# A hybrid decoder layer in float32: the first three weight blocks in ten pieces, and the unread matmuls on a constant

## The chip, the cores and the metric

The kernel runs on one core of a Trainium2 chip. The core has five engines that work side by side, each with its own instruction stream: TensorE (PE in the profile; its weight loads are shown apart as PEld), VectorE (DVE), ScalarE (ACT), GpSimd (POOL) and SyncE (SP), which here only issues transfers. Sixteen transfer engines move data between the device's memory and the on-chip memory. The metric is the device time of one execution in microseconds (us). The median of three runs is 1709.07 us (1709.02 to 1709.25).

## The reference

One layer of a decoder for 256 prompt tokens and 8 x 4 sample tokens, T = 288 rows of 2048 features, in float32:

```python
z = jnp.einsum('ntd,de->nte', x, w_in)
h, gate_b, gate_c, q, k, v, g_a, g_b = jnp.split(z, _split_points(), axis=-1)
ya = gate_b * causal_dwconv(gate_c * h)
yb = dilated windowed attention of q, k, v in 3 groups of 4 heads, merged
mixed = jax.nn.sigmoid(g_a) * (ya @ w_branch_a) + jax.nn.sigmoid(g_b) * (yb @ w_branch_b)
x1 = _layernorm(ALPHA * x + mixed @ w_out, ln1_g, ln1_b)
a, b = jnp.split(x1 @ w_up, 2, axis=-1)
y = _layernorm(ALPHA * x1 + (jax.nn.silu(causal_dwconv(a)) * b) @ w_down, ln2_g, ln2_b)
```

The lines for `ya`, `yb` and the convolution in `y` are shortened here. The key and value caches and the convolution states are returned as well. Nearly all the work is in the products with the weights: the weights are read once each, and the page counts 427.50 MB read in all.

## The kernel before

**Products.** Features lie on the 128 partitions. A weight matrix is cut into blocks of 128 output features; a block is 16 k-tiles (`KD`) of 128 x 128. So that TensorE keeps float32 accuracy, each operand is split into a rounded part `hi` and a remainder `lo` (`split`, line 248: ScalarE casts `hi`, VectorE subtracts to get `lo`). One k-tile of one block is then three matmuls of 288 columns: hi by hi, hi by the lo of x, and the lo of the weights by hi (`mms`, lines 243 to 245). A block is 48 matmuls.

**The usual stream of blocks.** `prepare` (line 185) issues the load of the next block from SyncE into the tile `wst` (three buffers) and splits it in two halves into `whi` and `wlo` (four buffers each). `product` (line 225) does a block. The first block that comes this way is called block 3 here; its load is issued in two halves (line 193).

**The front.** Blocks 0, 1 and 2 of the input projection don't go that way, since at the start both x and the weights are still on their way. Blocks 0 and 1 are loaded together into `w_two` (shown as the tile dd, its hi as yal, its lo as cache), block 2 into `w_one` (wst, whi, wlo), x into `xs` (yah, its hi as xh, its lo as xl). The front is cut into 8 pieces of two k-tiles (`N_PIECE`). For each piece three transfers are issued, x, `w_two`, `w_one` (lines 277 to 286), x from ScalarE's queue for the first two pieces and from SyncE's afterwards. ScalarE's table load is placed between its two (line 281, a copy of two columns of zeros). Then the casts and subtractions are written out and held in this order on ScalarE and VectorE (`casts`, `rests`, lines 287 to 310). In the first piece, x is cast one k-tile at a time, and VectorE does the cast of `w_two`, one k-tile at a time. `first_three` (line 314) runs the 144 matmuls of the three blocks piece by piece, in an order that is held: for each of the three terms, blocks 0 and 1, then block 2. `behind` (line 144) adds an order between two instructions of one engine.

**The unread matmuls.** Ahead of all this, TensorE runs `N_WARM` = 17 matmuls whose result nobody reads (line 261). They read a tile of zeros that VectorE writes (line 258).

**Behind the front** come the loads of block 3 (two halves), block 4, the constants (`cst`) and so on, all issued by SyncE (lines 195, 751, 390, 391).

Of the kernel before, what the change touches and what calls it, by code (L numbers as in the profile page):

```python
# [10 lines left out]
F32 = mybir.dt.float32  # L11
F32R = mybir.dt.float32r
# [5 lines left out]
P = 128  # L18
D = 2048
KD = D // P  # L20
# [3 lines left out]
T = SEQ + NS  # L24
# [8 lines left out]
HK = KD // 2  # L33
# [39 lines left out]
N_CT = 18  # L73
N_REST = 48

N_PIECE = 2

N_WARM = 17


PACE = 12, 13
# [19 lines left out]
def layer_kernel(ctx: ExitStack, tc: tile.TileContext, ins, outs):  # L101
    nc = tc.nc
    pe, dve, act, pool, sp = nc.tensor, nc.vector, nc.scalar, nc.gpsimd, nc.sync
# [3 lines left out]
    wk = ctx.enter_context(tc.tile_pool(name="wk", bufs=2))  # L107
    ps = ctx.enter_context(tc.tile_pool(name="ps", bufs=5, space=PSUM))
# [3 lines left out]
    def nm(s):  # L112
        uid[0] += 1
        return f"{s}_{uid[0]}"

    def sb(pl, shape, tag, dt=F32, bufs=None):
        return pl.tile(shape, dt, tag=tag, name=nm(tag), bufs=bufs)

    def acc(half=H):
        return sb(ps, [P, half, 2], "acc")  # L120
# [4 lines left out]
    def h3(ap):  # L125
        return ap.rearrange("p k (h a) -> p k h a", h=2)
# [8 lines left out]
    def f32(ap):  # L135
        return ap.bitcast(F32)
# [7 lines left out]
    def behind(i, after):  # L144

        tc.add_manual_dep(i.ins, after.ins.name, no_sync, reason="pace")
# [38 lines left out]
    def prepare():  # L185
        src, nk = next(w_left, (None, 0))
        if nk == 0:
            return
        st = sb(wp, [P, KD, P], "wst")
        src = src.rearrange("p (k c) -> p k c", c=P)  # L190
        loads[0] += 1

        for k0 in range(0, nk, HK if loads[0] == 1 else nk):
            k = slice(k0, k0 + (HK if loads[0] == 1 else nk))
            d = sp.dma_start(st[:, k, :], src[:, k])
        n = loads[0]
        w_load[0] = d
        if n >= 20 and n % 10 in (0, 3, 7):
            copy_rest(d)
        w_ready.append([half_block(st, k0, min(HK, nk - k0)) for k0 in range(0, nk, HK)])  # L200
# [24 lines left out]
    def product(x):  # L225

        w = w_ready.pop(0)
        if not w_ready:
            prepare()
        if steps_on[0]:  # L230
            next(steps, None)
        o = acc(x[0].shape[-1])
        mms(o, w, x)
        prompt_step()
        return o.rearrange("p a h -> p h a")
# [12 lines left out]
    def split(hi, lo, src):  # L248
        return act.copy(hi, src), dve.tensor_tensor(lo, src, f32(hi), ALU.subtract)  # L249

    ones_d = sb(big, [P, P], "ones_d", F32R)
    ones_p = sb(big, [P, P], "ones_p", F32R)
    pool.memset(f32(ones_d), 1.0 / D)
    pool.memset(f32(ones_p), 1.0 / P)


    zero = sb(wk, [P, T], "cy", F32R, bufs=2)
    dve.memset(f32(zero), 0.0)
    o = sb(ps, [P, T], "acc")
    for _ in range(N_WARM):  # L260
        pe.matmul(o, zero[:, :P], zero, start=True, stop=True)


    xh = sb(big, [P, KD, HX], "xh", F32R)[:, :, : 2 * HG].rearrange("p k (h a) -> p k h a", h=2)
# [1 line left out]
    x_in = ins["x"].rearrange("p (k t) -> p k t", t=T)  # L266
    xs = sb(big, [P, KD, T], "yah")
# [6 lines left out]
    w_one = sb(wp, [P, KD, P], "wst")  # L274
    w_one_hi, w_one_lo = ([sb(wp, [P, HK, P], n, F32R, bufs=4) for _ in range(2)] for n in ("whi", "wlo"))
    w_in_one = ins["w_in"][2].rearrange("p (k c) -> p k c", c=P)
    for k0 in range(0, KD, N_PIECE):
        k = slice(k0, k0 + N_PIECE)
        if k0 == N_PIECE:

            i_table = act.copy(sb(wk, [P, 2], "wgb", bufs=2), f32(zero[:, :2]))
        i_x = (act if k0 <= N_PIECE else sp).dma_start(xs[:, k], x_in[:, k])
        if k0 == N_PIECE:
            behind(i_x, i_table)
        sp.dma_start(w_two[:, :, k], w_in_two[:, :, k])
        sp.dma_start(w_one[:, k], w_in_one[:, k])
    casts, rests = [], []
    for k0 in range(0, KD, N_PIECE):
        k = slice(k0, k0 + N_PIECE)
        h = slice(k0 % HK, k0 % HK + N_PIECE)  # L290
        parts = (
            (xh[:, k, :, :H], xl[:, k, :, :H], xs[:, k].rearrange("p k (a h) -> p k h a", h=2)),
            (w_two_hi[:, :, k], w_two_lo[k0 // HK][:, :, h], w_two[:, :, k]),
            (w_one_hi[k0 // HK][:, h], w_one_lo[k0 // HK][:, h], w_one[:, k]),
        )
        for n, (hi, lo, src) in enumerate(parts):
            if k0 or n == 2:
                casts.append(act.copy(hi, src))
            else:

                for c in range(N_PIECE):
                    e = (slice(None),) * (1 + n) + (slice(c, c + 1),)
                    if n == 0:
                        casts.append(act.copy(hi[e], src[e]))
                    else:
                        rests.append(dve.tensor_copy(hi[e], src[e]))
        rests += [dve.tensor_tensor(lo, src, f32(hi), ALU.subtract) for hi, lo, src in parts]
    for row in (casts, rests):
        for before, i in zip(row, row[1:]):
# [4 lines left out]
    def first_three():  # L314

        prepare()
        o = [acc() for _ in range(3)]

        def first_w(lo, b, k):
            if b < 2:  # L320
                return w_two_lo[k // HK][:, b, k % HK] if lo else w_two_hi[:, b, k]
            return (w_one_lo if lo else w_one_hi)[k // HK][:, k % HK]

        before = None
        for k0 in range(0, KD, N_PIECE):
            for term in range(3):
                for blocks in ((0, 1), (2,)):
                    for k in range(k0, k0 + N_PIECE):
                        xk = x[term == 1][:, k].rearrange("p h a -> p a h")
                        for b in blocks:  # L330
                            i = pe.matmul(  # L331
                                o[b], first_w(term == 2, b, k), xk,
                                start=k == 0 and term == 0, stop=k == KD - 1 and term == 2,
                            )
                            if before is not None:
                                behind(i, before)
                            before = i
        return [t.rearrange("p a h -> p h a") for t in o]
# [23 lines left out]
    n = NH * NG * SEQ  # L362
# [373 lines left out]


    q_first = first_three()
    for j in range(NH):
        for g in range(NG):  # L740
# [12 lines left out]
    for j in range(NH):  # L753
        kT, vT = (kv[:, j % 2, c] for c in range(2))
        k_class = []
        for g in range(NG):
            for t in (kT, vT):
                o = product(x).rearrange("p h a -> p a h")
# [54 lines left out]
    for i in range(KD):  # L813
        ph = product(x)
        h = sb(wk, [P, T], "h", bufs=2)
# [19 lines left out]
    for i in range(KD):  # L835
# [3 lines left out]
        o = product((h3(yah), h3(yal)))  # L839
# [6 lines left out]
    for i in range(KD):  # L846
# [3 lines left out]
        o = product((h3(ybh), h3(ybl)))  # L850
# [182 lines left out]
    for i in range(KD):  # L1033
        o = product((h3(mxh), h3(mxl)))
# [35 lines left out]
    for part, nf in enumerate(THIRDS):  # L1070
# [42 lines left out]
        for i in range(KD):  # L1113
            o = product((h3(gh), h3(gl)))
# [209 lines left out]
```

## Time and profile before

| | |
|---|---|
| median of the runs | 1709.07 us |
| profiled execution, its own time | 1709.05 us |
| its span, first to last instruction | 1707.3 us |
| granted TensorE clock, mean | 0.999 |
| TensorE busy | 1699.9 us, 14148 matmuls |
| VectorE, ScalarE, GpSimd busy | 1192.2, 941.3, 387.6 us |
| moved by the transfer engines | 436.16 MB, 255 GB/s on average |
| transfer time, share of 16 engines' span, main queue | 67.6% |

How to read the rows that follow. A row of the timeline gives the start and the length in us, the engine, the line of the kernel, the operation, the tile written and the tiles read, the shape and the count of instructions that were merged into the row; in square brackets stands how long the engine had been idle before it, and what ended that. SPq and ACTq are the queues' own instructions, the issues of transfers. A row of the stretches gives for each engine the busy time and, in parentheses, the number of instructions. "us to landing" is the time from the start of an issue to the arrival of the last byte's signal. Sizes with KB are in units of 1024 bytes.

### The profile page before, as it was taken

How to read it: one execution, taken by the hardware profiler on the slowest of the kernel's cores; microseconds unless marked ns; L12 is line 12 of the kernel's file. 1: busy time of each engine (PE TensorE's matmuls, PEld its weight loads, DVE VectorE, ACT ScalarE, POOL GpSimd, SP SyncE). 2: the span in 40 equal slices, each digit the busy share in tenths (PEclk: the TensorE clock that was granted, in tenths of full speed). 3: DMA queues.
4: the chain of work that ended last, by engine and by line, in shares of the span. 5: the costliest groups of instructions: out<-in, count | busy, mean ns of one | idle time of the engine just before them, and what ended most of it. 6: DMA issues, size and time to landing. Idle time of an engine off the chain costs nothing.

```text
span 1707.3 us, 34334 instructions
## 1 busy us (share of the span) xinstructions
PE 1699.9 (100%) x14148; PEld 1694.4 (99%) x14148; DVE 1192.2 (70%) x1575; ACT 941.3 (55%) x1665; POOL 387.6 (23%) x510
## 2 busy tenths in 40 slices
PE   9999999999999999999999999999999999999998
PEld 9999999999999999999999999999999999999998
DVE  5477889978887675455788887855686554555575
ACT  5578876645666564444546555543555443344454
POOL 1123333202222210001453332300111100011164
PEclk9999999999999999999999999999999999999999
DMA  8788877676778886677766666666666566666663
GB/s 297 287 298 316 335 304 265 235 280 249 272 292 335 326 310 249 222 261 253 274 236 226 228 247 230 229 233 222 228 231 257 222 229 238 249 223 231 223 242 135
DMA packets 59068, 436.16 MB, mean 255 GB/s; under 512 B 7648, under 2 KB 11232, under 8 KB 19168
## 3 DMA queue, kind: packets, MB, share of 16 engines
q1 hardware_dynamic: 57472, 429.85, 67.6%
q10 hardware_dynamic: 1440, 4.13, 0.7%
q8 instruction: 110, 1.80, 0.4%
q14 instruction: 46, 0.38, 0.1%
HBM read 427.50 MB, written 94.53 MB: 306 GB/s over the span
## 4 chain that ended last, share of the span: by engine, by line
PE 98%; ACT 1%; DVE 1%; DMA 0%; issue 0%; SPq 0%; DVEq 0%
PE acc L243 32%; PE acc L245 32%; PE acc L244 32%; PE acc L331 1%; DMA wst<-in_w_in 0%; ACT yal L458 0%; DVE wlo L249 0%; PE acc L439 0%; PE att L478 0%; ACT yah L458 0%; ACT whi L249 0%; DVE dd L570 0%; PE long L978 0%; DVE yah L990 0%; PE acc L985 0%
## 5 line engine op out<-in xcount | busy, mean ns | idle before, releaser
L249 DVE TENSOR_TENSOR wlo<-wst,whi 128x1024 fp32r<-128x1024 f32 (+1 forms) x578 | 738.1, 1280 | 405.2 <-ACT whi L249 402.1
L249 ACT CAST whi<-wst 128x1024 fp32r<-128x1024 f32 (+1 forms) x578 | 588.6, 1021 | 679.9 <-PE acc L244 611.0
L243 PE MATMUL acc<-xh,whi 128*128 128x288 f32 (+1 forms) x3216 | 921.1, 286 | 0.0
L245 PE MATMUL acc<-xh,wlo 128*128 128x288 f32 (+1 forms) x3216 | 920.5, 286 | 0.4 <-DVE wlo L249 0.4
L244 PE MATMUL acc<-xl,whi 128*128 128x288 f32 (+1 forms) x3216 | 920.3, 286 | 0.0
L243 PEld LDWEIGHTS acc<-xh,whi 128*128 128x128 f32 x3216 | 607.8, 189 | 1.3 <-issue 1.2
L245 PEld LDWEIGHTS acc<-xh,wlo 128*128 128x128 f32 x3216 | 607.8, 189 | 0.8 <-DVE wlo L249 0.8
L244 PEld LDWEIGHTS acc<-xl,whi 128*128 128x128 f32 x3216 | 607.8, 189 | 0.0
L245 PE MATMUL acc<-yah,wlo 128*128 128x288 f32 x1216 | 347.7, 286 | 0.0
L244 PE MATMUL acc<-yal,whi 128*128 128x288 f32 x1216 | 347.7, 286 | 0.0
L243 PE MATMUL acc<-yah,whi 128*128 128x288 f32 x1216 | 347.6, 286 | 0.0
L245 PEld LDWEIGHTS acc<-yah,wlo 128*128 128x128 f32 x1216 | 229.8, 189 | 0.0
L244 PEld LDWEIGHTS acc<-yal,whi 128*128 128x128 f32 x1216 | 229.8, 189 | 0.0
L243 PEld LDWEIGHTS acc<-yah,whi 128*128 128x128 f32 x1216 | 229.8, 189 | 0.0
L794 POOL COPY qk_s<-u 128x2 f32<-128x2 f32 x44 | 36.8, 836 | 535.5 <-ACT u L1083 412.7
L782 DVE SCALAR_TENSOR_TENSOR cy<-u,prm,cy 128x304 f32<-128x304 f32 x120 | 72.6, 605 | 5.6 <-ACT cy L780 2.4
L564 POOL TENSOR_TENSOR cache<-cache,dd 128x1024 f32<-128x1024 f32 x16 | 34.1, 2134 | 93.4 <-DMA cache<-in_cv 55.8
L249 ACT CAST yah<-ya 128x288 fp32r<-128x288 f32 x76 | 32.6, 429 | 27.5 <-DVE ya L805 11.1
L564 POOL TENSOR_TENSOR cache<-cache,qk_s 128x1024 f32<-128x1024 f32 x16 | 32.7, 2045 | 53.7 <-DMA cache<-in_ck 40.6
L853 POOL TENSOR_TENSOR ya<-ya,dd 128x288 f32<-128x288 f32 x16 | 13.7, 858 | 133.8 <-DVE ya L852 132.8
L775 POOL COPY u<-prm 128x16 f32<-128x16 f32 x60 | 42.2, 704 | 4.6 <-DMA prm<-in_prm 4.6
L562 ACT ACTIVATE cache<-cache,qk_s 128x128 f32<-128x128 f32 x128 | 40.8, 392 | 0.0
(224 smaller groups left out, 1190.8 us busy)
## 6 DMA issues: line engine op xcount, KB each, us to landing
wst<-in_w_in SPq DMA_DIRECT2D x112, 1024.0 KB, 5.0
wst<-in_w_up SPq DMA_DIRECT2D x88, 1024.0 KB, 4.9
wst<-in_w_down SPq DMA_DIRECT2D x32, 1024.0 KB, 4.9
cache<-in_ck SPq DMA_DIRECT2D x18, 1024.0 KB, 7.8
cache<-in_cv SPq DMA_DIRECT2D x18, 1024.0 KB, 8.5
wst<-in_w_a SPq DMA_DIRECT2D x16, 1024.0 KB, 4.9
wst<-in_w_out SPq DMA_DIRECT2D x16, 1024.0 KB, 4.9
wst<-in_w_down SPq DMA_DIRECT2D x16, 768.0 KB, 4.4
```

The costliest lines, as they stand in the source:

```text
L243: pe.matmul(out, hi[:, c, :], xh_k, start=k == 0, stop=False)
L244: pe.matmul(out, hi[:, c, :], xl_k, start=False, stop=False)
L245: last_mm[0] = pe.matmul(out, lo[:, c, :], xh_k, start=False, stop=k == nk - 1)
L249: return act.copy(hi, src), dve.tensor_tensor(lo, src, f32(hi), ALU.subtract)
L331: i = pe.matmul(o[b], first_w(term == 2, b, k), xk, start=k == 0 and term == 0, stop=k == KD - 1 and term == 2,)
L562: behind(act.activation(o[:, a, b], t[:, a, b], AF.Copy, scale=w[:, a, b : b + 1]), w_split[0])
L564: behind(pool.tensor_tensor(o, t, w.unsqueeze(3).broadcast_to([P, *n]), ALU.mult), w_split[1])
L775: pool.tensor_copy(tail[:, :, 0:2], prm[:, state : state + 2 * NB].rearrange("p (b r) -> p b r", b=NB))
L782: dve.scalar_tensor_tensor(y, u[:, i : i + YW], prm[:, w0 + i : w0 + i + 1], y, ALU.mult, ALU.add)
L794: pool.tensor_copy(dst[:, 0:2], u[:, SEQ : SEQ + 2])
L853: pool.tensor_tensor(m, m, ma[:, i], ALU.add)
```

## The change

The front gets ten pieces, given as first k-tile and number of k-tiles: four of one k-tile, then six of two. All loops over the front go over this list. In the first piece, which is one k-tile now, x is cast in one instruction, and the cast of `w_two` stays on VectorE; all other casts are on ScalarE as before. The first two pieces' x is issued by ScalarE, the others' by SyncE. A piece of one k-tile takes x in rows of 1152 bytes and weights in rows of 512 bytes a partition, where a piece of two has 2304 and 1024. There are 30 transfers in place of 24.

The unread matmuls, now 15, read a constant zero that the program's preamble keeps in one column, with a step of zero over 128 and 288 columns. They stand ahead of GpSimd's two memsets in the program; VectorE's memset is gone. The copy that goes with the table load reads the same constant.

```diff
-N_PIECE = 2
-
-N_WARM = 17
+PIECES = (0, 1), (1, 1), (2, 1), (3, 1), (4, 2), (6, 2), (8, 2), (10, 2), (12, 2), (14, 2)
+
+N_WARM = 15
...
+    zero = nc.const_aps.tensor(0.0, [P, 1], F32)
+    zeros = [zero.bitcast(F32R).broadcast_to([P, n]) for n in (P, T)]
+    o = sb(ps, [P, T], "acc")
+    for _ in range(N_WARM):
+        pe.matmul(o, *zeros, start=True, stop=True)
     ones_d = sb(big, [P, P], "ones_d", F32R)
     ones_p = sb(big, [P, P], "ones_p", F32R)
     pool.memset(f32(ones_d), 1.0 / D)
     pool.memset(f32(ones_p), 1.0 / P)
-
-
-    zero = sb(wk, [P, T], "cy", F32R, bufs=2)
-    dve.memset(f32(zero), 0.0)
-    o = sb(ps, [P, T], "acc")
-    for _ in range(N_WARM):
-        pe.matmul(o, zero[:, :P], zero, start=True, stop=True)
...
-    for k0 in range(0, KD, N_PIECE):
-        k = slice(k0, k0 + N_PIECE)
-        if k0 == N_PIECE:
-
-            i_table = act.copy(sb(wk, [P, 2], "wgb", bufs=2), f32(zero[:, :2]))
-        i_x = (act if k0 <= N_PIECE else sp).dma_start(xs[:, k], x_in[:, k])
-        if k0 == N_PIECE:
+    for n, (k0, nk) in enumerate(PIECES):
+        k = slice(k0, k0 + nk)
+        if n == 1:
+
+            i_table = act.copy(sb(wk, [P, 2], "wgb", bufs=2), zero.broadcast_to([P, 2]))
+        i_x = (act if n <= 1 else sp).dma_start(xs[:, k], x_in[:, k])
+        if n == 1:
             behind(i_x, i_table)
         sp.dma_start(w_two[:, :, k], w_in_two[:, :, k])
         sp.dma_start(w_one[:, k], w_in_one[:, k])
     casts, rests = [], []
-    for k0 in range(0, KD, N_PIECE):
-        k = slice(k0, k0 + N_PIECE)
-        h = slice(k0 % HK, k0 % HK + N_PIECE)
+    for k0, nk in PIECES:
+        k = slice(k0, k0 + nk)
+        h = slice(k0 % HK, k0 % HK + nk)
...
         for n, (hi, lo, src) in enumerate(parts):
-            if k0 or n == 2:
+            if k0 or n != 1:
                 casts.append(act.copy(hi, src))
             else:
-
-                for c in range(N_PIECE):
-                    e = (slice(None),) * (1 + n) + (slice(c, c + 1),)
-                    if n == 0:
-                        casts.append(act.copy(hi[e], src[e]))
-                    else:
-                        rests.append(dve.tensor_copy(hi[e], src[e]))
+                rests.append(dve.tensor_copy(hi, src))
         rests += [dve.tensor_tensor(lo, src, f32(hi), ALU.subtract) for hi, lo, src in parts]
...
-        for k0 in range(0, KD, N_PIECE):
+        for k0, nk in PIECES:
             for term in range(3):
                 for blocks in ((0, 1), (2,)):
-                    for k in range(k0, k0 + N_PIECE):
+                    for k in range(k0, k0 + nk):
```

## The prediction

> **What bounds the kernel now.** I read the page first, for its span, its busy shares and its chain.
>
> ```profile
> span 1707.3 us, 34334 instructions
> PE 1699.9 (100%) x14148; PEld 1694.4 (99%) x14148; DVE 1192.2 (70%) x1575; ACT 941.3 (55%) x1665; POOL 387.6 (23%) x510
> ...
> PE 98%; ACT 1%; DVE 1%; DMA 0%; issue 0%; SPq 0%; DVEq 0%
> ```
>
> TensorE holds 98% of the chain, so the change can only act through the moment from which TensorE runs without a break. The stretches of the front show that moment (columns: stretch and its length, busy time and count of each engine, granted clock, DMA share, GB/s).
>
> ```profile
> 0.00:1.22 1.22, 0.00 (x1) 0.00 (x1) 0.30 (x1) 0.02 (x1) 0.62 (x8) 1.00 0.00 0
> 1.22:5.60 4.38, 4.31 (x18) 4.12 (x18) 0.44 (x3) 2.26 (x4) 0.00 (x0) 1.00 0.85 235
> 5.60:6.79 1.19, 0.73 (x4) 0.51 (x5) 1.19 (x3) 0.46 (x2) 0.00 (x0) 1.00 1.12 382
> 6.79:24.04 17.25, 17.25 (x140) 17.25 (x141) 13.66 (x25) 13.67 (x24) 0.15 (x1) 1.00 1.07 385
> ```
>
> The 17 unread matmuls fill 1.22 to 5.60, four real ones run, TensorE waits, and from 6.79 the other 140 of the 144 of `first_three` run to 24.04: 17.25/140 = 0.123 us each. Had all 144 run so, they would have begun at 24.04 - 144 x 0.1225 = 6.40. I call this the effective start. The chain of waits over the first 8 us says what sets it:
>
> ```profile
> 1.24 5.07 DMA wst<-in_w_in
> 6.31 0.02 issue
> 6.33 0.41 ACT whi L298
> 6.75 0.04 issue
> 6.79 1.25 PE acc L331 x8
> ```
>
> It is the landing of the first piece of `w_one` at 6.31, then its cast. After that the transfers stay close behind. ScalarE's timeline (start, length, what, idle time before it) shows this:
>
> ```profile
> 4.70 0.81 ACT L304 CAST xh<-yah 128x288 fp32r<-128x288 f32 x2 [2.02 <-DMA yah<-in_x]
> 6.33 0.40 ACT L298 CAST whi<-wst 128x256 fp32r<-128x256 f32 x1 [0.82 <-DMA wst<-in_w_in]
> 6.64 0.72 ACT L298 CAST xh<-yah 128x576 fp32r<-128x576 f32 x1
> ...
> 13.83 0.77 ACT L298 CAST xh<-yah 128x576 fp32r<-128x576 f32 x1 [0.20 <-DMA yah<-in_x]
> ...
> 15.72 0.76 ACT L298 CAST xh<-yah 128x576 fp32r<-128x576 f32 x1 [0.20 <-DMA yah<-in_x]
> ...
> 19.11 0.73 ACT L298 CAST xh<-yah 128x576 fp32r<-128x576 f32 x1 [1.72 <-DMA yah<-in_x]
> ...
> 21.50 1.04 ACT L249 CAST whi<-wst 128x1024 fp32r<-128x1024 f32 x1 [0.71 <-DMA wst<-in_w_in]
> ```
>
> Every piece waits for its x, and pieces come 15.72 - 13.83 = 1.89 us apart: the transfer engines, not TensorE (2 x 9 x 0.1225 = 2.2 us a piece), pace this queue. The next weights (block 3, line 195) stand in the same queue. Their first half is cast at 21.50, when it lands, and is subtracted on VectorE; the third matmul of block 3 reads the result:
>
> ```profile
> 22.58 2.50 DVE L249 TENSOR_TENSOR wlo<-wst,whi 128x1024 fp32r<-128x1024 f32 x2 [1.01 <-ACT whi L249]
> ```
> ```profile
> 24.17 0.19 PEld L245 LDWEIGHTS acc<-xh,wlo 128*128 128x128 f32 x1
> ```
> ```profile
> L249 DVE TENSOR_TENSOR wlo<-wst,whi x12: 1212/1224/1342, 22.6 to 48.7; 128x1024 fp32r<-128x1024 f32 x12
> ```
>
> The first of the two subtractions ends at 22.58 + 1.22 = 23.80, and the load of the weights begins at 24.17. With 0.04 us of hand-over (22.58 after the cast's end at 22.54) **the slack is 24.17 - 23.84 = 0.33 us**. This small number decides my forecast: an earlier front is worth no more than 0.33 us unless block 3 lands earlier too.
>
> **The change, part by part.** *The unread matmuls.* They now read a constant that is written in the preamble, so they no longer wait for VectorE.
>
> ```profile
> 0.24 0.10 POOL L1311 MEMSET const-float32-0.0<- 128x1 f32 x1 [0.24 <-issue]
> ...
> 0.73 0.20 POOL L253 MEMSET ones_d<- 128x128 f32 x1 [0.29 <-POOLq L1311]
> ```
> ```profile
> 0.87 0.30 DVE L258 MEMSET cy<- 128x288 f32 x1 [0.87 <-PEq L1311]
> ```
> ```profile
> 1.22 4.31 PE L261 MATMUL acc<-cy 128*128 128x288 f32 x17 [1.22 <-DVE cy L258]
> 5.60 0.73 PE L331 MATMUL acc<-xh,yal 128*128 128x288 f32 x4
> ```
>
> They can start when the other engines do, at 0.73 to 0.87 instead of 1.22, some 0.4 us earlier. Each takes 4.31/17 = 0.25 us, twice the later 0.1225, though the clock column reads 1.00 throughout; the four real ones behind them are nearly at full speed ((0.73 - 0.29)/3 = 0.15). Two fewer save 0.5 us: 15 end near 0.8 + 15 x 0.25 = 4.6. None lies on the path, as the first real operands come later. No row shows a matmul whose operands repeat one column; from below the price is zero, from above I take the longest of the unread ones, unpipelined, 0.607 us in the row below: 0.8 + 15 x 0.607 = 9.9 as their end. I take zero, because these are the same instruction with the same counts, and only the step differs.
>
> ```profile
> L261 PE MATMUL acc<-cy x17: 305/442/607, 1.2 to 5.2; 128*128 128x288 f32 x17
> ```
>
> *The small pieces at the front.* The queue's price per packet comes from two stretches, one of front pieces, one of whole blocks:
>
> ```profile
> DMA packets 2233, 2.75 MB, mean 366 GB/s; under 512 B 190, under 2 KB 1721, under 8 KB 2233
> ```
> ```profile
> DMA packets 407, 2.09 MB, mean 418 GB/s; under 512 B 45, under 2 KB 45, under 8 KB 209
> ```
>
> The first is 8.2 to 15.7 (16 engines x 7.5 us / 2233 = 53.7 ns a packet of 1232 B on average), the second 20 to 25 (80 us / 407 = 197 ns, 5135 B). A line through both is 8.6 ns a packet plus 0.0366 ns a byte. For the first piece, 480 of 960 KB stand before the end of its `w_one` (x of two pieces, `w_two`, `w_one`), in as many packets: 480 x 1024 x 0.0366 / 16 = 1.12 us earlier, a landing at 5.19. The cast of 128 columns is 0.27 (0.40 for 256, 0.72 for 576: 1 ns a column), so the first tile's third matmul starts at 5.50, two matmuls done before it: effective start 5.26, **1.1 us earlier**. Behind it ScalarE casts one tile at a time, 0.40 + 0.40 + 0.27 = 1.07 us against 1.10 of matmuls; it only just keeps up, so I count on 0.75 and keep 1.1 as the other end.
>
> The same four tiles cost the queue. Their weights go in 512-byte runs instead of 1024, x in 1152 instead of 2304: 256 more packets a tile, 1024 in all, and 6 more transfers with 16 completion packets each: 1120 x 8.6 / 16 = **0.60 us later for everything behind them**, block 3 included. From below this is 0 (only bytes count), from above 1120 x 53.7 / 16 = 3.8 us (only packets count). I take 0.60; the two stretches fix it.
>
> The Trainium skill speaks against this step: "DMA: Bandwidth & Descriptors" (Specifications) sets 512 B as the smallest transfer at line rate, so 512-byte runs would lose nothing; that is rival A below. The two stretches disagree already at 1024 and 2304 B: 366 against 418 GB/s.
>
> *Issue.* x came from ScalarE for the first two pieces before, too, so nothing changes engines; SyncE issues 28 transfers instead of 22.
>
> ```profile
> 4.70 0.33 SPq L286 DMA_DIRECT2D wst<-in_w_in  x1
> 5.15 0.38 SPq L282 DMA_DIRECT2D yah<-in_x  x1
> 6.33 0.38 SPq L285 DMA_DIRECT2D dd<-in_w_in  x1
> ```
>
> These are the 9th to 11th transfers; they start at the landings of the first three (x 4.70, `w_two` about 5.15, `w_one` 6.31). So eight are outstanding at once. In the new front eight hold 944 KB, or 2.6 us at 366 GB/s, against a shortest landing of 1.9:
>
> ```profile
> yal<-in_cst SPq DMA_DIRECT2D x4, 64.0 KB, 1.9
> ```
>
> So the queue should not run dry; if it does, SyncE's 0.33 to 0.47 us an issue gives at worst 1.3 us a tile against 0.94, over three tiles 1 us more. I take zero.
>
> *The casts of the first piece* move only with the piece. POOL's two memsets move behind the unread matmuls in program order, on another engine, and nobody in the front reads them.
>
> **The sum.** TensorE reaches block 3 at 24.04 - 0.75 = 23.29. Block 3's first half lands at 21.48 + 0.60, its subtraction ends at 24.40, and the load may begin at 24.44 instead of 24.17: **+0.27 us**. The 0.75 is swallowed by a wait of about a microsecond at block 3's third matmul. Behind that nothing passes the delay on: from 24.04 to 40.00 TensorE is busy without a gap,
>
> ```profile
> 24.04:40.00 15.96, 15.96 (x133) 15.96 (x132) 6.69 (x9) 6.85 (x14) 3.68 (x8) 1.00 0.62 213
> ```
>
> at a DMA share of 0.62, so the queue catches up there. The profiled execution took 1709.05 us (span 1707.3, and 1.75 around it), the median of the runs is 1709.07; 1709.05 + 0.27 = **1709.3**. About 0.2%, 3.4 us, is what a measurement can tell from no change: the forecast is no change.
>
> **The rivals.**
>
> *A: the runs of 512 B cost only their bytes.* Then block 3 lands when it does now and the slack caps the gain: -0.33, 1708.7. For it: nothing but bytes would matter; against it the two stretches. If moreover block 3 lands earlier, the lead itself is left, -0.75 to -1.1: 1708.0 to 1708.3. That could come from the one late engine:
>
> ```profile
> q8 instruction: 1, 0.02, 3.6%
> ```
>
> one instruction fetch (0.02 MB) shares the queue at 15.5 to 17.5, after which the x of the last piece is 1.72 us late instead of 0.20. Were it to fall elsewhere, block 3 would land up to 1.5 us earlier.
>
> *B, slower: TensorE is slow again.* The unread matmuls end at 4.6, the real ones begin near 5.2, and the half speed needs up to 4.3 us of unbroken work to go (1.22 to 5.5 above). If the gap counts as a break, the next 4.3 us run at half speed and lose 2.15: less the lead of 0.75, block 3 starts 1.4 us later than now, 1710.4. It decides from a loss of 0.75 + 0.27 = 1.02 us, eight or nine slow matmuls. For it: two fewer unread matmuls and an earlier start of them; against: the wait before 6.79 cost no speed.
>
> The Trainium skill ("TensorE: Matmul & The Clock Gate", Part 1: The HAM clock gate) has a free-running window of about 3.4 us that must be busy; by that an estimate of the loss is 1.7, and the time 1710.0.
>
> *C, slower: the queue runs dry or packets cost more than 8.6 ns.* Block 3 lands 1.0 us later on top, or up to 3.8 in all: 1710.3 to 1712.5.
>
> *D, slower: repeated columns read slowly*, 9.9 as the end of the unread ones: effective start 3.5 later than 6.40, 1712.6. Nothing in the profile speaks for it.
>
> **How the numbers follow.** Forecast (wait at block 3, 1709.0 to 1709.8) 0.50; A 0.20, of which 0.06 with the late engine gone; B 0.15; C 0.10; D 0.03; 0.02 for an order of instructions that changes further on. The range 1708.2 to 1711.0 leaves out the end of A with the full lead, the upper half of C and D. Only C's end, D and a changed order pass 3.4 us: slower 0.06, faster 0.03, the same 0.91.
>
> **What would show it.** Right: the first real matmul near 5.1 instead of 5.60; the first `w_one` cast near 5.2; pieces of two tiles still 1.9 us apart; the first cast of line 249 near 22.1; TensorE idle for some 1 us before the third matmul of block 3, with VectorE's subtraction (line 249) as releaser. Wrong: line 249's cast at 21.5 or before (A), real matmuls 0.25 us apart after 5.2 (B), DMA share under 1 between 5 and 10 us (C), unread matmuls beyond 5 us (D). A difference that arises behind 40 us would make the whole argument wrong.

## The result, and the profile after

| | before | after |
|---|---|---|
| median of 22 runs each, side by side | 1709.20 us (1707.76 to 1709.52) | 1711.47 us (1710.63 to 1712.86) |
| ratio, with its 95% interval | | 1.0015 (1.0009 to 1.0021) |
| profiled execution, its own time | 1709.05 us | 1711.30 us |
| its span | 1707.3 us | 1709.2 us |

The changed kernel is 0.15% slower. That is inside the 0.2% that the forecast called no change, but 2.3 us instead of +0.3, and outside the range, whose upper end was 1711.0. The last matmul of the profiled execution starts at 1703.82 instead of 1702.08, 1.74 us later. All of that arises in the first 45 us. Of the 2.25 us between the two own times 0.35 lies outside the span (2.1 us around it instead of 1.75) and some 0.2 behind the last matmul; neither was looked into.

TensorE's timeline of the new front shows the start and the first real matmuls, then the two long waits:

```profile
0.77 3.94 PE L255 MATMUL acc<-const-float32-0.0 128*128 128x288 f32 x15 [0.77 <-PEq L1303]
4.50 0.80 PE L323 MATMUL acc<-xh,yal 128*128 128x288 f32 x2
...
9.48 0.29 PE L323 MATMUL acc<-xh,wlo 128*128 128x288 f32 x1
11.32 0.76 PE L323 MATMUL acc<-xh,yal 128*128 128x288 f32 x4 [1.55 <-ACT yal L296]
...
14.13 0.76 PE L323 MATMUL acc<-xh,yal 128*128 128x288 f32 x4 [0.34 <-ACT yal L296]
```

The first real matmul runs at 4.50, 1.1 us earlier than before (5.60). Then TensorE works off the four small pieces and stands still ahead of the first piece of two k-tiles, until 11.32, and again ahead of the second, until 14.13. The stretches put sizes to that (columns as in the prediction):

```profile
4.50:9.60 5.10, 5.10 (x37) 5.05 (x36) 3.74 (x12) 3.08 (x10) 0.00 (x0) 1.00 0.93 253
9.60:11.32 1.72, 0.17 (x3) 0.00 (x1) 0.62 (x1) 1.36 (x3) 0.00 (x0) 1.00 0.84 264
11.32:25.26 13.94, 13.60 (x108) 13.38 (x109) 10.63 (x19) 10.33 (x18) 0.15 (x1) 1.00 1.03 380
```

The 36 matmuls of the small pieces take 5.10 us instead of 36 x 0.1225 = 4.41, because the first few run at half speed: 0.69 lost. The wait costs 1.72. The other 108 take 13.94 instead of 13.23: 0.71 lost, of which 0.51 is the wait before 14.13 (the piece before it ends at 13.62). Together 3.12 us, and the 144 are through at 25.26: 4.50 + 17.64 + 3.12. The effective start is 25.26 - 17.64 = 7.62, so the front is **1.22 us later** than the 6.40 of before, where 0.75 to 1.1 earlier was forecast.

The same stretches side by side tell where the bytes went, before first:

```profile
4.00:8.00 4.00, 3.47 (x21) 3.06 (x21) 2.71 (x6) 2.48 (x6) 0.00 (x0) 1.00 1.07 379
8.00:12.00 4.00, 4.00 (x35) 4.00 (x34) 3.85 (x8) 3.55 (x8) 0.00 (x0) 1.00 1.09 366
```

and after:

```profile
4.00:8.00 4.00, 4.00 (x26) 3.91 (x26) 3.33 (x11) 3.17 (x10) 0.00 (x0) 1.00 0.94 243
8.00:12.00 4.00, 2.45 (x20) 2.24 (x19) 2.16 (x6) 2.02 (x5) 0.00 (x0) 1.00 0.89 277
```

From 4 to 12 us the queue moves 243 and 277 GB/s instead of 379 and 366, 0.90 MB less. The DMA share is under 1 there. That is the sign the prediction had named for rival C. For the first of the two stretches SyncE's timeline shows why:

```profile
4.22 0.43 SPq L280 DMA_DIRECT2D yah<-in_x  x1
...
5.69 0.43 SPq L280 DMA_DIRECT2D yah<-in_x  x1
```

SyncE issues without a pause, three issues in 5.69 - 4.22 = 1.47 us, 0.49 each. A small piece is three issues and 144 + 128 + 64 = 336 KB: 344 kB / 1.47 us = 234 GB/s is all that SyncE can order, and 243 is what moved. A piece of two k-tiles gives 468 by the same sum, more than the engines carry.

The orders explain the first stretch and not the second. Summed over the packets of the traces, the bytes that are ordered and not yet moved are 0.44 to 0.98 MB from 4 to 7.5 us in the changed kernel, but 1.1 to 1.5 MB from 8 to 12, about what the kernel before has throughout (1.2 to 1.6). What differs is a few single packets: from 4 to 12 us 30 packets of the changed kernel (14 of them from 8 on) take over 0.25 us each, the longest 1.05, and only one does before (0.68). A landing counts when the last of its sixteen signals is in. Those of the x issued at 5.69 come from 8.21 to 9.94, spread over 1.73 us; before, the signals of each x that is issued in the first 9 us are spread over 0.82 to 0.85. That the long packets spread them is likely and not shown, and why they take so long, no run shows.

The x of the first larger piece, issued at 5.69, lands at 9.94, where the chain of waits has `DMA yah<-in_x` from 5.69 for 4.25 us; ScalarE's cast of it and of its weights leads to 11.32.

Everything behind it in the queue is late too. ScalarE's cast of block 3's first half, and TensorE at block 3:

```profile
23.20 1.04 ACT L249 CAST whi<-wst 128x1024 fp32r<-128x1024 f32 x1 [0.69 <-DMA wst<-in_w_in]
```
```profile
25.56 0.39 PE L245 MATMUL acc<-xh,wlo 128*128 128x288 f32 x1
25.79 0.29 PE L243 MATMUL acc<-xh,whi 128*128 128x288 f32 x1
...
43.19 0.29 PE L244 MATMUL acc<-xl,whi 128*128 128x288 f32 x1
43.55 0.39 PE L245 MATMUL acc<-xh,wlo 128*128 128x288 f32 x1
```

and before, block 3's fourth matmul:

```profile
24.41 0.29 PE L243 MATMUL acc<-xh,whi 128*128 128x288 f32 x1
```

The cast runs at 23.20 instead of 21.50, **1.70 us later** where 0.60 was forecast. There is luck in that figure: of this transfer's sixteen signals, fifteen are in at 22.42 instead of 19.85, 2.57 us later. The last one trails them by 1.63 us before and by 0.76 after; in both traces an instruction fetch shares the queue just ahead (from 16.29 and from 19.30). Block 3's third matmul waits a little (25.56 starts 0.05 late, and the next comes 0.23 behind it instead of 0.12), so block 3's fourth stands at 25.79 against 24.41: +1.38. A last wait, for another subtraction of line 249, comes at 43.2, from 43.19 to 43.55 with 0.10 more behind it: +0.34, hence +1.72. From there to the last matmul the two traces run in step.

### The profile page after: what moved, and what is told of

Same layout as the page of the kernel before. It is cut to its first block, busy times and chain, and to the rows that moved or that the text cites. A ratio compares the mean times of both kernels' runs of the same rounds, so it can differ in the third digit from the quotient of the medians.

```text
span 1709.2 us, 34350 instructions
## 1 busy us (share of the span) xinstructions
PE 1700.7 (100%) x14146; PEld 1694.8 (99%) x14146; DVE 1196.4 (70%) x1579; ACT 942.1 (55%) x1670; POOL 383.0 (22%) x510
## 4 chain that ended last, share of the span: by engine, by line
PE 96%; DMA 2%; ACT 1%; DVE 1%; SPq 0%; issue 0%; DVEq 0%; ACTq 0%
PE acc L243 32%; PE acc L245 32%; PE acc L244 32%; DMA wst<-in_w_in 1%; DMA yah<-in_x 0%; DMA dd<-in_w_in 0%; DVE wlo L249 0%; ACT whi L249 0%; ACT yal L450 0%; PE acc L431 0%; PE att L470 0%; ACT yah L450 0%; SPq L382 0%; DVE dd L562 0%; PE long L970 0%
## 5 line engine op out<-in xcount | busy, mean ns | idle before, releaser
L774 DVE SCALAR_TENSOR_TENSOR cy<-u,prm,cy 128x304 f32<-128x304 f32 x120 | 77.8, 648 | 5.6 <-ACT cy L772 2.4
```

Source lines behind the costliest of these rows:

```text
L774: dve.scalar_tensor_tensor(y, u[:, i : i + YW], prm[:, w0 + i : w0 + i + 1], y, ALU.mult, ALU.add)
```

## The experiments

Each was timed beside the kernel before on the same chip. Ratios have their 95% interval.

**1. The unread matmuls alone.** The kernel before, with 15 unread matmuls on the constant and the old pieces.

```diff
-N_WARM = 17
+N_WARM = 15
...
+    zero = nc.const_aps.tensor(0.0, [P, 1], F32)
+    zeros = [zero.bitcast(F32R).broadcast_to([P, n]) for n in (P, T)]
+    o = sb(ps, [P, T], "acc")
+    for _ in range(N_WARM):
+        pe.matmul(o, *zeros, start=True, stop=True)
...
-    dve.memset(f32(zero), 0.0)
```

> The kernel before, with only the unread matmuls changed (15 on the constant, no memset by VectorE). Theory (the loss is in the transfers of the small pieces): the first piece lands as before, TensorE reaches block 3 at 24.0 us, time within 0.3 us of the kernel before (1709.2). Rival B (half speed returns because the unread matmuls end at 4.5, a microsecond before the first real ones): real matmuls 0.25 us apart after 5.6, 1 to 2 us slower, 1710.2 to 1711.2.

Measured: 1710.72 against 1709.35, ratio 1.0006 (0.9997 to 1.0015). The 11 runs fall into two groups, three at 1709.2 to 1709.3 and eight at 1710.2 to 1711.2. The profiled one (1710.93) belongs to the upper group. TensorE's timeline of it:

```profile
0.77 3.59 PE L255 MATMUL acc<-const-float32-0.0 128*128 128x288 f32 x15 [0.77 <-PEq L1311]
5.63 0.73 PE L331 MATMUL acc<-xh,yal 128*128 128x288 f32 x4 [1.27 <-ACT xh L304]
6.81 0.51 PE L331 MATMUL acc<-xh,whi 128*128 128x288 f32 x2 [0.45 <-ACT whi L298]
7.16 1.05 PE L331 MATMUL acc<-xl,yal 128*128 128x288 f32 x4
```

and its stretches:

```profile
7.20:10.65 3.45, 3.45 (x17) 3.45 (x16) 3.32 (x7) 3.24 (x7) 0.00 (x0) 0.51 1.08 369
10.65:14.10 3.45, 3.45 (x29) 3.45 (x29) 3.12 (x7) 2.99 (x7) 0.00 (x0) 1.00 1.08 365
```

The 15 end near 4.4, 1.3 us before the first real operands, since the old first piece lands no earlier than it did. Four real matmuls then run fast, TensorE waits 0.45 us more, and from 7.2 to 10.65 the clock column reads 0.51: 17 matmuls where the next stretch of the same length has 29. That is the mechanism of rival B. It costs 12 x 0.1225 = 1.5 us. The theory of the expectation (within 0.3 us of before) holds in three runs, its rival B (1710.2 to 1711.2) in eight.

**2. The pieces alone.** The changed kernel with the old 17 unread matmuls on VectorE's zeros (the edit of experiment 1 backwards).

> The changed kernel with the old unread matmuls (17, VectorE's zeros). Theory: the stall at the first piece of two tiles stays, time within 0.5 us of the changed kernel (1711.5). Rival B: the half-speed matmuls at the start are gone and at least 1 us of the loss with them, 1710.5 or less.

Measured: 1710.95 against 1709.35, 1.0009 (1.0000 to 1.0018). The trace has 237 and 269 GB/s from 4 to 12 us, the wait ahead of the first two-tile piece (1.24 in the timeline, up to 11.78), and block 3's cast at 22.49. So the pieces carry most of the loss with either kind of unread matmuls: 1.60 us of it is left where the changed kernel loses 2.27, between the two expectations. Block 3's cast is 0.7 us earlier than in the changed kernel, with the same transfers. With one profile of each kernel, that 0.7 us can't be given a cause.

**3. Two small pieces instead of four.**

```diff
-PIECES = (0, 1), (1, 1), (2, 1), (3, 1), (4, 2), (6, 2), (8, 2), (10, 2), (12, 2), (14, 2)
+PIECES = (0, 1), (1, 1), (2, 2), (4, 2), (6, 2), (8, 2), (10, 2), (12, 2), (14, 2)
```

> The changed kernel with two pieces of one tile instead of four (nine pieces). Theory (SyncE's three issues of 0.48 us a tile feed the queue too slowly while the pieces are small, and it runs dry): pieces of two tiles follow after six issues, the queue stays full, no wait of TensorE over 0.3 us at the first piece of two tiles, block 3 lands about 0.3 us later than before instead of 1.7, 1708.8 to 1709.6. Rival (each small packet costs, whatever the queue): half of the loss stays, 1710.3.

Measured: 1710.12 against 1709.35, 1.0006 (0.9997 to 1.0015). No wait had been expected, but there was one:

```profile
7.07 0.29 PE L323 MATMUL acc<-xh,wlo 128*128 128x288 f32 x1
9.13 0.64 PE L323 MATMUL acc<-xh,yal 128*128 128x288 f32 x3 [1.77 <-ACT yal L296]
```

The two small pieces are used up at 7.19 and the first larger one is ready at 9.13. The queue moves 269 GB/s from 4 to 8 us and 381 from 8 to 12: six small transfers are enough to leave it short, only earlier and for less long. Block 3's cast comes at 22.08. The time lies nearer to the rival's 1710.3 than to the theory's 1708.8 to 1709.6, though in the trace the loss is the wait.

**4. Small pieces in the casts and matmuls, large ones in the transfers.** The changed kernel, whose loop over the transfers goes by two k-tiles again.

```diff
-    for n, (k0, nk) in enumerate(PIECES):
-        k = slice(k0, k0 + nk)
+    for n, k0 in enumerate(range(0, KD, 2)):
+        k = slice(k0, k0 + 2)
```

> The changed kernel with its ten pieces of casts and matmuls, but the eight transfers of two tiles that the kernel before has. Theory (the loss is in the transfers): the first real matmul waits for a landing at 6.3 again, no stall of more than 0.3 us later, time within 0.5 us of the kernel before, 1708.9 to 1709.7. Rival (the casts of one tile, 1.07 us a tile on ScalarE, hold TensorE up): more than 1 us slower than before.

Measured: 1710.68 against 1709.35, 1.0007 (0.9998 to 1.0016), again in two groups: four runs at 1709.0 to 1709.5, seven at 1710.7 to 1711.3. The profiled run (1709.46) is of the lower group. It moves 380 and 368 GB/s from 4 to 12 us, has block 3's cast at 21.51 as before (21.50) and no wait behind 7 us. So in this run shorter casts and matmuls cost nothing, and the transfers are what matters. The upper group takes the median out of the expected 1708.9 to 1709.7; it lies where that of experiment 1 does, and the unread matmuls again end 0.9 us or more ahead of the first real ones; no profile of that group was taken here.

**5. The packets alone.** The kernel before, with the weights of block 2 laid out in `wst` so that each run of a partition is 512 bytes: 1024 packets more, in the same 24 transfers.

```diff
-    w_one = sb(wp, [P, KD, P], "wst")
+    w_one = sb(wp, [P, KD, P], "wst").rearrange("p (a h) c -> p h a c", a=N_PIECE)
...
-        sp.dma_start(w_one[:, k], w_in_one[:, k])
+        sp.dma_start(w_one[:, k0 // N_PIECE], w_in_one[:, k])
...
-            (w_one_hi[k0 // HK][:, h], w_one_lo[k0 // HK][:, h], w_one[:, k]),
+            (w_one_hi[k0 // HK][:, h], w_one_lo[k0 // HK][:, h], w_one[:, k0 // N_PIECE]),
```

> The kernel before, with block 2's first weights stored so that all its eight transfers go in runs of 512 B instead of 1024: 1024 packets more, as many as the change adds, but no transfer more and no piece smaller. Theory: the queue is full, so the price is my 8.6 ns a packet, block 3 lands 0.55 us later (22.0 instead of 21.5) and the fourth matmul of block 3 starts about 0.2 us later than 24.41; time within 0.4 us of before. Rival (small packets are the loss): block 3 lands 1.7 us later as with the change, 1711.

Measured: 1709.38 against 1708.86, 1.0003 (0.9994 to 1.0013). Stretches, ScalarE and TensorE of its trace:

```profile
8.00:12.00 4.00, 4.00 (x35) 4.00 (x34) 3.75 (x8) 3.44 (x7) 0.00 (x0) 1.00 1.10 352
```
```profile
21.92 1.05 ACT L249 CAST whi<-wst 128x1024 fp32r<-128x1024 f32 x1 [0.76 <-DMA wst<-in_w_in]
```
```profile
24.28 0.39 PE L245 MATMUL acc<-xh,wlo 128*128 128x288 f32 x1
24.50 0.29 PE L243 MATMUL acc<-xh,whi 128*128 128x288 f32 x1
```

352 GB/s instead of 366, with the DMA share full. Block 3's cast is 0.42 us later, which is 0.42 x 16 / 1024 = 6.6 ns a packet (8.6 was forecast; by the fifteenth of the sixteen signals, 20.38 against 19.85, it would be 8.3). Its fourth matmul is 0.09 later, 24.50 against 24.41: 0.42 less the slack of 0.33. So the packets are dearer than their bytes, and they make a quarter of the 1.70.

**6. Four small pieces in the middle.** The same number of pieces, packets and transfers as in the changed kernel, at k-tiles 4 to 7.

```diff
-PIECES = (0, 1), (1, 1), (2, 1), (3, 1), (4, 2), (6, 2), (8, 2), (10, 2), (12, 2), (14, 2)
+PIECES = (0, 2), (2, 2), (4, 1), (5, 1), (6, 1), (7, 1), (8, 2), (10, 2), (12, 2), (14, 2)
```

> The changed kernel with its four pieces of one tile moved from tiles 0 to 3 to tiles 4 to 7; as many transfers and packets as the change. Theory: when the small pieces come, the queue holds 1.8 MB, SyncE is ahead, nothing runs dry; no wait of TensorE over 0.3 us at tile 8, block 3 lands 0.6 to 1.0 us later than before. Rival (small packets or casts, wherever they stand): block 3 lands 1.7 us later and TensorE waits at tile 8. The clock can add a window of half speed, seen as matmuls 0.24 us apart.

Measured: 1712.19 against 1708.86, 1.0019 (1.0010 to 1.0029). The expectation was that the transfers already ordered, 1.8 MB, would cover the small ones. They didn't: by the packets of the trace only 0.53 to 0.57 MB were ordered and not yet moved from 7.5 to 9 us, since no more than eight transfers are outstanding and the small ones fill these places. The stretches, and SyncE's timeline:

```profile
8.00:12.00 4.00, 4.00 (x35) 4.00 (x34) 4.00 (x13) 3.81 (x13) 0.00 (x0) 1.00 0.99 254
12.00:16.00 4.00, 3.05 (x25) 2.83 (x24) 1.13 (x4) 1.30 (x3) 0.00 (x0) 1.00 0.96 275
```
```profile
7.99 0.47 SPq L284 DMA_DIRECT2D wst<-in_w_in  x1
...
9.45 0.47 SPq L284 DMA_DIRECT2D wst<-in_w_in  x1
```

A piece in 1.46 us again (9.45 - 7.99), 236 GB/s ordered and 254 moved. The hole moves with the small pieces: TensorE waits at 16.30, ahead of the next large one (1.25 in its timeline), and block 3's cast runs at 23.72. So it is not the start of the kernel that is slow; small transfers are, wherever they stand. Here too the second stretch is slow with 1.1 to 1.3 MB outstanding.

**7. Smaller transfers, nothing else.** The kernel before, whose six transfers of the first two pieces are cut into two of 64 partitions each. The rows of each partition, the casts and the matmuls stay the same.

```diff
-        i_x = (act if k0 <= N_PIECE else sp).dma_start(xs[:, k], x_in[:, k])
+        at = (slice(0, P // 2), slice(P // 2, P)) if k0 <= N_PIECE else (slice(0, P),)
+        for h in at:
+            i_x = (act if k0 <= N_PIECE else sp).dma_start(xs[h, k], x_in[h, k])
...
-        sp.dma_start(w_two[:, :, k], w_in_two[:, :, k])
-        sp.dma_start(w_one[:, k], w_in_one[:, k])
+        for h in at:
+            sp.dma_start(w_two[h, :, k], w_in_two[h, :, k])
+        for h in at:
+            sp.dma_start(w_one[h, k], w_in_one[h, k])
```

> The kernel before, with each of the six transfers of the first two pieces cut into two of 64 partitions: twelve transfers of half the size, the same packets and the same pieces for the casts. Theory (issue rate and eight outstanding transfers): 0.45 us an issue at half the bytes lets the queue run dry between 4 and 8 us as in the changed kernel, DMA under 300 GB/s there instead of 370 to 390, and block 3 lands 0.7 to 1.5 us later. Rival (packet size): the same rate and the same landing as before, 21.5.

Measured: 1712.34 against 1708.86, 1.0021 (1.0012 to 1.0031). Stretches and SyncE:

```profile
4.00:8.00 4.00, 1.83 (x11) 1.38 (x10) 1.36 (x4) 1.19 (x4) 0.00 (x0) 0.96 0.86 197
8.00:12.00 4.00, 3.94 (x20) 3.94 (x21) 2.57 (x6) 2.44 (x6) 0.00 (x0) 0.62 0.78 223
```
```profile
0.73 1.51 SPq L288 DMA_DIRECT2D dd<-in_w_in  x2
...
3.68 1.29 SPq L288 DMA_DIRECT2D dd<-in_w_in  x2
6.55 1.13 SPq L290 DMA_DIRECT2D wst<-in_w_in  x2
```

197 and 223 GB/s with the old rows and the old pieces: the size and number of the transfers alone is enough. Here an issue takes 0.57 to 0.76 us, and between 4.97 and 6.55 SyncE waits 1.6 us for a landing. Block 3's cast runs at 26.12, 4.6 us later than before, where 0.7 to 1.5 was expected. This profiled run (1714.43) is the slowest of the ten by 1.7 us. Part of its loss is that its first piece is itself late (first real matmul at 7.08) and that half speed follows (0.62 in the clock column from 8 to 12); the size of the rest is not explained.

**8. x of the third and fourth piece from ScalarE.** The changed kernel with two issues fewer on SyncE.

```diff
-        i_x = (act if n <= 1 else sp).dma_start(xs[:, k], x_in[:, k])
-        if n == 1:
+        i_x = (act if n <= 3 else sp).dma_start(xs[:, k], x_in[:, k])
+        if 1 <= n <= 3:
```

> The changed kernel, x of the third and fourth piece issued by ScalarE too. SyncE has two issues fewer ahead of the first piece of two tiles, which it issues about 0.5 us earlier than 5.69. Theory: that piece's x lands 0.5 to 1 us earlier than 9.94 and the wait of 1.7 us there shrinks by as much; block 3 lands 0.3 to 0.8 us earlier than 23.2. Rival (packet size): both unchanged within 0.2 us.

Measured: 1710.92 against 1708.86, 1.0012 (1.0003 to 1.0022); no relief, against the expectation. SyncE's timeline:

```profile
2.23 0.47 SPq L284 DMA_DIRECT2D wst<-in_w_in  x1
3.74 0.38 SPq L283 DMA_DIRECT2D dd<-in_w_in  x1
...
5.15 0.47 SPq L284 DMA_DIRECT2D wst<-in_w_in  x1
6.63 0.33 SPq L280 DMA_DIRECT2D yah<-in_x  x1
```

Now SyncE stands still twice for a landing (2.70 to 3.74, 5.62 to 6.63), and x of the first large piece is issued at 6.63, later than 5.69. The limit has changed: it is the number of transfers outstanding instead of the time of an issue. Block 3's cast at 23.18 is where it was.

**9. One small piece in front.** Two k-tiles of the list are single, the first and one later, to keep the halves of the weights whole.

```diff
-PIECES = (0, 1), (1, 1), (2, 1), (3, 1), (4, 2), (6, 2), (8, 2), (10, 2), (12, 2), (14, 2)
+PIECES = (0, 1), (1, 2), (3, 2), (5, 2), (7, 1), (8, 2), (10, 2), (12, 2), (14, 2)
```

> The changed kernel with its ten pieces cut to nine: one tile first, then three pieces of two tiles, one of one, and four of two. Theory (small transfers run the queue dry, and the next x then comes slowly): only the first three transfers are small, 1.55 MB are issued by 3.7 us, the queue stays full, DMA at 350 GB/s or more from 4 to 16 us, x packets slow only before 4 us, block 3 lands within 0.4 us of before (21.5) instead of 23.2. Rival (the changed code of the front, whatever the transfers): block 3 still lands more than 1 us late. The time itself hangs on the clock, since TensorE waits for the second piece: 1709 to 1711.

Measured: 1708.52 (1708.08 to 1709.53) against 1709.10, 0.9998 (0.9989 to 1.0007). Stretches, ScalarE and TensorE:

```profile
4.00:8.00 4.00, 3.88 (x24) 3.52 (x24) 2.98 (x8) 2.69 (x7) 0.00 (x0) 1.00 1.05 360
8.00:12.00 4.00, 4.00 (x35) 4.00 (x34) 3.95 (x9) 3.28 (x8) 0.00 (x0) 1.00 1.08 358
```
```profile
20.95 1.05 ACT L249 CAST whi<-wst 128x1024 fp32r<-128x1024 f32 x1 [0.87 <-DMA wst<-in_w_in]
```
```profile
23.09 0.29 PE L243 MATMUL acc<-xh,whi 128*128 128x288 f32 x1
...
23.54 0.29 PE L243 MATMUL acc<-xh,whi 128*128 128x288 f32 x1
```

The queue stays full, block 3 starts at 23.09, 0.95 earlier than before, and its fourth matmul at 23.54, 0.87 earlier. That is more than the slack of 0.33 allows, because block 3's cast is 0.55 earlier (a landing within 0.4 of before was expected). That part looks like luck and not like the change: thirteen of the sixteen signals of block 3's first half are in at 19.77, as before (19.79), and only the last one, which trails behind the instruction fetch, comes earlier (20.93 instead of 21.48). It is what rival A had named for the late engine. The profiled run took 1708.08, below the expected 1709 to 1711, but seven of the 27 runs of the kernel before lie at 1708.0 to 1708.3 too, and the time can't be told from no change.

**10. 20 unread matmuls.** Experiment 1 with 20 instead of 15.

> The run with only the unread matmuls changed, but 20 of them on the constant instead of 15, so that they reach to the first real ones at 5.6. If the half speed there came from the gap of 1.3 us behind the unread matmuls: no real matmul 0.24 us apart after 7 us, all runs within 0.5 us of the kernel before, none near 1711. If it came from the constant or from the earlier start: the half speed stays, and two groups of times as before.

Measured: 1709.09 (1708.15 to 1709.29) against 1709.10, 1.0000 (0.9992 to 1.0009). The upper group of experiment 1 is gone, with the same constant. So the half speed there comes from the gap behind the unread matmuls, not from what they read. The two experiments ran on different chips, but experiment 7, on the chip of this one and with the old zeros, shows half speed behind a gap as well (2.01 us in its timeline).

**11. The slack alone.** The kernel before, with x of the second piece issued by SyncE behind the first weights, and block 3's first half cast and subtracted in quarters, so that its third matmul needs less of it.

```diff
-        i_x = (act if k0 <= N_PIECE else sp).dma_start(xs[:, k], x_in[:, k])
-        if k0 == N_PIECE:
-            behind(i_x, i_table)
+        (act if k0 == 0 else sp).dma_start(xs[:, k], x_in[:, k])
...
-        w_split[:] = split(hi[:, :n, :], lo[:, :n, :], st[:, k0 : k0 + n, :])
+        n_cast = 4 if loads[0] == 1 else n
+        for c in range(0, n, n_cast):
+            at = slice(c, c + n_cast)
+            w_split[:] = split(hi[:, at, :], lo[:, at, :], st[:, k0 + c : k0 + c + n_cast, :])
```

> The kernel before with x of the second piece issued by SyncE behind the first piece's weights, and the first half of block 3 cast and subtracted in quarters of four tiles. Theory: the first w_one lands 0.8 to 1.1 us earlier than 6.31, no transfer is smaller, block 3 lands as before, its first lo is ready 1.2 us earlier; TensorE is at block 3 0.4 to 0.8 us earlier than 24.04, 1708.3 to 1708.8. If the slack at block 3 were not the bound, the quarters would change nothing; if x of the second piece is late, TensorE waits there and the time stays.

Measured: 1708.64 (1708.31 to 1708.92) against 1709.10, 0.9998 (0.9989 to 1.0007). Block 3 starts at 23.67 and its fourth matmul at 24.04, without a wait and 0.37 earlier than before, the whole lead of its front. The quarters are not shown to be needed for it: in this profile block 3's cast begins at 20.86, 0.64 earlier than before, since the last of the sixteen signals trails less again (20.84 behind a fifteenth at 19.89), and that alone would have freed the slack. In time it can't be told from no change either.

## Why the prediction was wrong, step by step

**The step that failed is the one on issue:** "So the queue should not run dry; if it does ... over three tiles 1 us more. I take zero." Both halves of its working were too kind. It set eight outstanding transfers (944 KB) against "a shortest landing of 1.9", from one load of 64 KB of the constants. In the new front the same size takes longer. The list of DMA issues of the changed kernel, over the first 9 us (KB each, median us to landing):

```profile
dd<-in_w_in SPq DMA_DIRECT2D x4, 128.0 KB, 3.2
...
yah<-in_x SPq DMA_DIRECT2D x2, 144.0 KB, 3.2
wst<-in_w_in SPq DMA_DIRECT2D x4, 64.0 KB, 2.9
```

Eight transfers of 344 / 3 = 115 kB on average in 3.2 us are an estimated 287 GB/s, under the 366 that the engines carry. And "0.33 to 0.47 us an issue" counted the issues without the 0.04 to 0.05 us between them and with the shortest ones: 1.47 us a piece instead of 1.3, 234 GB/s. Either limit leaves the queue short while the small pieces are on their way. Experiment 8 lifts the one and meets the other, experiment 7 shows that smaller transfers do it without any other edit, experiment 6 that another place only moves the hole, experiment 3 that two small pieces make a smaller one, experiment 4 that nothing else in the pieces costs, and experiment 9 that one small piece at a time is carried. What follows had no term in the sum either: the long packets, with which the queue stays slow from 8 to 12 us although it holds enough again. At block 3 both together are 1.70 - 0.42 x 1120 / 1024 = 1.24 us where zero was taken, by single profiles and with the luck of the last signal in it. The short queue is the first half of rival C, to which the prediction gave one chance in ten; it named block 3 as the place, whereas the larger part of the loss is TensorE's own wait in the front (1.72 + 0.51).

**The lead at the start came, and larger than forecast.** The first real matmul was forecast near 5.1 and came at 4.50, the first cast of `w_one` near 5.2 and came at 4.24; why a whole microsecond earlier was not looked into. The lead was lost afterwards: TensorE works off a small piece in 9 x 0.1225 = 1.10 us where SyncE takes 1.47 to order one, and the x of the first larger piece then took 4.25 us to land.

**The unread matmuls cost what was taken:** 15 in (4.50 - 0.77) / 15 = 0.249 us each, against 0.25 before, with a column that repeats. Rival D falls.

**The price of a packet was right** within a third (6.6 ns against 8.6), and rival A falls with experiment 5. The Trainium skill's figure in "DMA: Bandwidth & Descriptors" (Specifications), 512 B as the smallest transfer at line rate, would have put experiment 5 at no loss; its 352 against 366 GB/s decides against it here, by 4%.

**The slack was right,** and it is the most solid number of the sum. From the start of block 3's first cast to its fourth matmul it is 2.59 us in the changed kernel (25.79 - 23.20), 2.58 in experiment 5 (24.50 - 21.92) and 2.59 in experiment 9 (23.54 - 20.95), wherever this chain binds. Before, it was 24.41 - 21.50 = 2.91, that is 0.33 more than needed: the 0.33 of the prediction.

**"Behind that nothing passes the delay on" was wrong by 0.34 us,** at 43.2. The share of 0.62 from which it was argued is a mean over 16 us; with block 3's data 1.70 late instead of 0.60, one subtraction was still late there. Without it the sum would be +1.38.

**Rival B is real, but not what decides here.** Experiment 1 shows its mechanism, half speed that returns behind a gap. In the profiled run of the changed kernel there is no such gap: the unread matmuls reach to the first real one, and the first five real ones, up to 5.81, still run at the half speed of the start, which makes the 0.69 us. Whether other runs of it lose more was not seen: what its runs lose beyond the 1.74 us of the trace (2.27 in the medians) is not placed.

**What stays open.** How the two limits and the long packets share the loss in the changed kernel. And where the long packets come from: from 8 to 12 us the changed kernel's DMA view has

```profile
DMA packets 916, 1.11 MB, mean 277 GB/s; under 512 B 74, under 2 KB 725, under 8 KB 916
```

and before, in the same stretch,

```profile
DMA packets 1206, 1.47 MB, mean 366 GB/s; under 512 B 105, under 2 KB 942, under 8 KB 1206
```

Both are packets of 1.2 kB on average, but the engines are busy 16 x 4 us x 0.89 / 916 = 62 ns with one instead of 16 x 4 x 1.09 / 1206 = 58. The packets don't all become slower: 14 of the 916 take over 0.25 us, and without these the mean is 55. From 4 to 12 us the traces of experiments 2, 3, 6, 7 and 8 have 19 to 47 such packets, experiment 9 has 16, and those of experiments 1, 4, 5, 10 and 11, whose first transfers are large and whole, have 0 to 3. So they come with the small transfers; that a thin queue is their cause is not shown.

## What to carry to other kernels

Before a transfer is cut, work out what the issuing engine can then order: bytes of a transfer over the time from one issue to the next, and the bytes that may be outstanding over the landing time that this stage shows, not a quiet one. If either is under what the transfer engines carry, the gain at the head comes back as a hole a few microseconds later; one small piece in front of large ones kept the queue full here (360 GB/s). An earlier start is worth only the slack of the next consumer that waits for the same queue, so measure that slack first. And where unread matmuls keep the clock up, let them reach to the first real one: an earlier or shorter stretch of them can cost more than it saves.

## What the hardware showed that was not expected

Half speed came back in experiment 1 after two short gaps, 1.27 us and 0.45 us with four real matmuls between; the profiled run is one of the eight slower ones of eleven. It lasted from 7.2 to 10.65, 3.45 us, with 0.51 in the clock column. The Trainium skill, "TensorE: Matmul & The Clock Gate" (Part 1: The HAM clock gate), has a free-running window of about 3.4 us, and the length agrees. Its advice on gaps ("Why this matters for your kernels": none over some 3 us) does not suffice here, since no gap was half as long.

The clock records of the traces say more. Full speed begins at another time in each profiled run, between 3.85 and 5.79 us with the same 15 unread matmuls. In experiments 1 and 7, 3.41 us after that moment half speed returns, for 3.41 us. Here are the 3.41 us ahead of it in experiments 1 and 7, and two such stretches with no half speed behind them, of experiment 4 and of the changed kernel:

```profile
3.85:7.26 3.41, 1.69 (x11) 1.28 (x11) 2.07 (x5) 1.71 (x4) 0.00 (x0) 1.00 1.08 383
4.23:7.65 3.42, 1.41 (x10) 1.15 (x9) 1.01 (x3) 0.84 (x3) 0.00 (x0) 1.00 0.92 213
4.64:8.05 3.41, 1.88 (x13) 1.62 (x13) 2.27 (x8) 2.12 (x7) 0.00 (x0) 1.00 1.07 378
9.20:12.61 3.41, 1.86 (x15) 1.65 (x14) 1.70 (x3) 1.61 (x3) 0.00 (x0) 1.00 0.91 292
```

TensorE is busy for 1.69 and 1.41 us where half speed follows, and for 1.86 us or more where it doesn't. All thirteen profiled runs fit this: counted in steps of 3.41 us from the start of full speed, a step decides by its whole busy time and not by its longest gap, with the boundary somewhere between 1.69 and 1.86 us, near half. No run was made to test it. It would also give the two groups of runs of experiment 1, since the steps fall differently from run to run. The step of the changed kernel from 9.20 lies close to the boundary, so some of its runs may lose speed there; that was not seen.

The other surprise is the scale: cutting six transfers into twelve, with the same rows of the same size (experiment 7), cost 1.0021 (1.0012 to 1.0031) of a kernel of 1.7 ms, as much as any change of the front tried here. In its profiled run the half speed is part of that.
